# Pairing the column chunks of the input projections anew in a two-layer decoder trunk

## Chip, cores, metric

One core of one Trainium2 chip runs the whole program. The metric is device time in microseconds (us), from the program's start to its end; the kernel before took 2420.99 us, the median of three runs (2418.62 to 2423.28).

## What is computed

The reference is a trunk of two layers on an input of 256 rows by 2048 channels, all in float32:

```python
for l in range(DEPTH):
    h = rms_norm(x, mix_norm[l])
    proj = h @ w_in[l]                       # 2048 -> 7680 columns: q | k | v | u, v of the gating unit | gate logits
    q, k, v, uv, gate_logits = jnp.split(proj, cuts, axis=-1)
    branch_a = sliding_window_attention(...q, k, v...) @ w_attn_branch[l]
    branch_b = chunked_sgu(jax.nn.gelu(uv), ...) @ w_sgu_branch[l]
    gates = jax.nn.sigmoid(gate_logits)
    merged = gates[..., :D_MODEL] * branch_a + gates[..., D_MODEL:] * branch_b
    x = x + merged @ w_out[l]
    h2 = rms_norm(x, ffn_norm[l])
    x = x + (jax.nn.silu(h2 @ w_gate[l]) * (h2 @ w_up[l])) @ w_down[l]
```

The case is about `proj`, whose 7680 columns are computed in 15 chunks of 512: one with keys and attention values (`kv` 0), two of queries (`q` 0, 1), two of the gating unit's `v` ("values", `v` 0, 1), two of its `u` (`u` 0, 1), and eight of gate logits (`gate` 0 to 7).

## The kernel before

**A product in three parts.** Every float32 operand is split into a high part and a remainder (`hi` and `lo` of a weight, `uh` and `ul` of an activation), and a product is the sum of high times high, high times remainder and remainder times high. `add_product` (L361, L362) issues these: 3 matmuls of 512 columns for each 128 rows of the contraction. ScalarE makes `hi` (L261), VectorE makes `lo` as the difference (L262).

**Entries.** The work of TensorE is a list of entries made before anything is issued. A usual entry is one weight tile of 256 contraction rows by 512 columns, used for both halves of the 256 activation rows: 2 x 2 x 3 = 12 matmuls. A chunk with contraction length 2048 is 8 such entries.

**Single or pair.** `single` makes a plan of one chunk: 8 entries, 96 matmuls. `pair` makes a plan of two chunks A and B. There the first two weight tiles of A and of B form a 2 x 2 block product with the activation halves, and that is computed by the scheme of Winograd and Strassen with 7 products in place of 8: entries P1, P5, P2, P6, P7, P4 (the head) and P3, with 6 matmuls each, 42 in place of 48. Four of them need a difference of weight tiles first (L246, a subtraction of whole tiles on VectorE), all seven need a split, and partial sums go through a tile called `kept`: ScalarE copies one bank out (L384), one bank to another (L385), VectorE adds to `kept` twice (L387), and ScalarE writes `kept` back into the banks of B (L390, two copies). The other six weight tiles of A (entries G) and of B (entries U) are usual entries. A pair is thus 7 x 6 + 12 x 12 = 186 matmuls in 19 entries; two singles are 192 matmuls in 16 entries.

**Order.** The six head entries of a pair are put between the last six entries of the plan ahead of it:

```python
order = [t[0], h[0], t[1], h[1], t[2], t[3], h[3], h[2], t[4], h[4], t[5], h[5]]
```

where `t` are those six and `h` is P1, P5, P2, P6, P7, P4. TensorE's order is fixed by the program; the order on the other engines is worked out by a planner that runs the program against a model of time, with edges that put some steps behind the newest weight split.

**Lead.** `Stream.next` runs ahead of TensorE: loads are asked for 7 entries ahead, splits are made 4 entries ahead, differences 6 entries ahead. There are 5 buffers for raw tiles of usual entries, one buffer for each of the four raw tiles of a block (`k11`, `k12`, `k21`, `k22`), and 4 buffers each for `hi` and `lo`.

**Steps by slots.** Everything else is hung on a clock of slots. A unit is one weight tile against 128 of the 256 activation rows, and a slot passes with every two units: one usual entry is a slot, a P entry is half a slot (`debt`). `after(n, fn)` runs a step n slots later. Queries: normalising and rotating them takes 5 steps on VectorE, then `turn` (L431) transposes 32 x 32 blocks on VectorE and moves them with 16 DMAs (L437), for keys and queries on the queue of SyncE (SP), the queue of all weight loads; ScalarE copies the result to `qT` (L791). Scores and value products of the attention have fixed slots after the first query chunk. Values (`Spatial.v`) are evicted by ScalarE (L878); 4 slots after `v` 1 comes a GELU over both chunks, then four normalising steps 6 slots apart. `Spatial.u` has its GELU 7 slots after `u` 1, and 3 and 9 slots later the mixing (`psg`, L942) reads the normalised values of chunk 0 and of chunk 1.

**Banks.** Plans of the input projection use four PSUM banks, two for A and two for B. A pair that follows a pair uses A's banks again as soon as they are evicted.

**First part.** `FIRST_PART` lists, for each layer, the plans of the first twelve chunks in order. Before, in layer 0: `kv` 0, `q` 0, `q` 1, `gate` 0, `v` 0, `v` 1 single, then (`gate` 1, `u` 0), (`u` 1, `gate` 2), (`gate` 3, `gate` 4). In layer 1 `q` 1 and `gate` 0 are a pair as well.

Of the kernel before, what the change touches and what calls it, by code (L numbers as in the profile page):

```python
# [54 lines left out]
U_GELU, U_MIX, U_TURN = 7, (3, 9), (32, 39)  # L55
VALUES = (34, 44), (54, 64)
LOAD_BY = (2, 4, 5, 5)
FIRST_PART = [[(("kv", 0),), (("q", 0),)] + early + [(("v", 0),), (("v", 1),), (("gate", 1), ("u", 0)), (("u", 1), ("gate", 2)),
                                                  (("gate", 3), ("gate", 4))]
              for early in ([(("q", 1),), (("gate", 0),)], [(("q", 1), ("gate", 0))])]  # L60


@with_exitstack
def hybrid_trunk(ctx: ExitStack, tc: tile.TileContext, x, mix_norm, w_in, q_norm, k_norm, sinks,
# [108 lines left out]
    for l in range(DEPTH):  # L173
        wl = w_in[l]

        def of_in(kind, c):
            o = {"kv": O_KV, "q": 0, "v": O_V, "u": O_U, "gate": O_GATE}[kind] + c * CW
            return wl[:, o:o + CW]

        for f in FIRST_PART[l]:  # L180
            plans.append((single if len(f) == 1 else pair)(("in", l), *(of_in(*c) for c in f)))
# [97 lines left out]
    def after(n, fn):  # L279
        steps.append((slot_no[0] + n, fn))  # L280
# [251 lines left out]
    def summed(units, c, at):  # L532

        uh, ul = units[c]
        flat = slot([P, 4, S], name="flat")
        nc.vector.tensor_tensor(out=flat, in0=uh.bitcast(F32), in1=ul.bitcast(F32), op=ALU.add)
        ss = slot([P, 4, 2, P], name="sums")  # L540
        a11, a12, a21, a22 = (flat[:, 2 * k:2 * k + 2, t * P:(t + 1) * P] for t in range(NT) for k in range(2))

        def sums(n):
            for o, x0, x1, op in ((0, a21, a22, ALU.add), (1, ss[:, 0], a11, ALU.subtract),
                                  (2, a11, a21, ALU.subtract), (3, a12, ss[:, 1], ALU.subtract))[2 * n:2 * n + 2]:
                nc.vector.tensor_tensor(out=ss[:, o], in0=x0, in1=x1, op=op)

        def finished():
            sh = slot([P, 4, 2, P], F32R, "sh")
            sl = slot([P, 4, 2, P], F32R, "sl")  # L550
            nc.scalar.activation(sh, ss, AF.Copy)
            nc.vector.tensor_tensor(out=sl, in0=ss, in1=sh.bitcast(F32), op=ALU.subtract)
            units[c] = (uh, ul, sh, sl)

        after(at[0], lambda: sums(0))
        after(at[1], lambda: sums(1))
        after(at[2], finished)
# [440 lines left out]
    for l in range(DEPTH):  # L998
# [29 lines left out]

        for chunks in FIRST_PART[l]:
            if chunks == FIRST_PART[l][-1]:  # L1030
                after(1, lambda: summed(att.attT, WINO, (1, 2, 4)))
# [108 lines left out]
```

## Time and profile before

| | |
|---|---|
| runs | 2418.62, 2420.99, 2423.28 us |
| profiled execution | span 2416.4 us from the first to the last instruction; the page gives no other time for it |
| mean granted TensorE clock | 1.000 |
| busy share | TensorE 100%, weight load 82%, VectorE 87%, ScalarE 63%, GpSimd 13% |
| matmuls | 10692 |
| HBM | 207 GB/s read over the span |

TensorE is PE in the rows, the loading of its weights PEld, VectorE DVE, ScalarE ACT, GpSimd POOL, and the sequencer of SyncE that issues the loads SPq. A group row ends with `busy, mean ns of one | idle time of the engine just before them, and what ended it`. A row of a stretch gives its length, then for each engine the busy time and how many instructions touch the stretch, the granted clock, the DMA share and GB/s. A row of waits gives us in total, how many, and the longest.

### The profile page before, as it was taken

To read this page: it belongs to the slowest core of one execution; us is meant where nothing else is said; L and a number is where in the kernel's file an instruction comes from. 1 tells how busy PE (TensorE), PEld (TensorE's weight loads), DVE (VectorE), ACT (ScalarE), POOL (GpSimd) and SP (SyncE) were. 2 spreads that over 40 slices of the span, in tenths; PEclk is the share of its full clock that TensorE was granted. 3 is DMA by queue.
4 is the path that set the end of the run, shared out by engine and by line. 5 is a ranking of instruction groups with operands and counts; after the bars stand their busy time and mean duration, and the time that the engine had idled before them with its cause. 6 is when DMAs were issued, how large, how long until landed. Compare 5 with 4: busy or idle time off the path is not lost.

```text
span 2416.4 us, 31069 instructions
## 1 busy us (share of the span) xinstructions
PE 2405.1 (100%) x10692; PEld 1970.7 (82%) x10692; DVE 2092.0 (87%) x2409; ACT 1532.4 (63%) x1932; POOL 303.4 (13%) x557
## 2 busy tenths in 40 slices
PE   9999999999999999999999999999999999999999
PEld 7877888888888888888888778888888888888887
DVE  7779787898999998799887897878889989998998
ACT  6477555576666675666665775555676666666665
POOL 1100001132110111001301000011311101110010
PEclk9999999999999999999999999999999999999999
DMA  8755678687677757776957557776867786677773
GB/s 287 233 167 164 178 204 251 221 264 239 191 238 228 239 179 223 245 225 178 293 177 260 174 160 197 215 223 227 269 219 232 213 258 204 199 231 229 235 223 138
DMA packets 285070, 527.16 MB, mean 218 GB/s; under 512 B 28208, under 2 KB 40080, under 8 KB 284912
## 3 DMA queue, kind: packets, MB, share of 16 engines
q1 hardware_dynamic: 263056, 486.36, 63.6%
q0 software_dynamic: 21536, 38.56, 6.2%
q8 instruction: 83, 1.36, 0.2%
q14 instruction: 75, 0.61, 0.1%
q10 hardware_dynamic: 320, 0.27, 0.0%
HBM read 483.66 MB, written 16.78 MB: 207 GB/s over the span
## 4 chain that ended last, share of the span: by engine, by line
PE 88%; DVE 4%; DMA 4%; issue 1%; ACT 1%; SPq 1%; POOL 0%; DVEq 0%; ACTq 0%
PE acc L361 58%; PE acc L362 29%; DVE wlo L262 2%; DMA raw<-in_w_up_dram 2%; DMA raw<-in_w_in_dram 1%; DMA tt<-box 1%; ACT whi L261 1%; DVE raw L246 1%; SPq L437 1%; PE psc L807 1%; PE po L859 0%; PE psg L942 0%; PE ppt L844 0%; PE pt L474 0%; POOL tt L437 0%
## 5 line engine op out<-in xcount | busy, mean ns | idle before, releaser
L261 ACT ACTIVATE whi<-raw 128x1024 fp32r<-128x1024 f32 (+1 forms) x1116 | 1166.6, 1058 | 786.3 <-PE acc L362 440.0
L262 DVE TENSOR_TENSOR wlo<-raw,whi 128x1024 fp32r<-128x1024 f32 (+1 forms) x1117 | 1343.5, 1216 | 269.3 <-ACT whi L261 255.3
L361 PE MATMUL acc<-whi,uh 128*128 128x512 f32 x2854 | 1116.7, 391 | 1.4 <-ACT uh L460 1.4
L361 PE MATMUL acc<-wlo,uh 128*128 128x512 f32 x2854 | 1113.3, 390 | 2.1 <-DVE wlo L262 1.3
L362 PE MATMUL acc<-whi,ul 128*128 128x512 f32 x2854 | 1112.1, 390 | 0.6 <-DVE ul L465 0.6
L361 PEld LDWEIGHTS acc<-wlo,uh 128*128 128x128 f32 x2854 | 536.0, 188 | 118.5 <-DVE wlo L262 6.6
L361 PEld LDWEIGHTS acc<-whi,uh 128*128 128x128 f32 x2854 | 535.9, 188 | 117.8 <-issue 4.9
L362 PEld LDWEIGHTS acc<-whi,ul 128*128 128x128 f32 x2854 | 535.9, 188 | 112.8 <-DVE ul L465 1.5
L437 POOL DMA_DIRECT2D tt<-box x464 | 228.0, 499 | 1202.6 <-DVE box L431 339.7
L246 DVE TENSOR_TENSOR raw<-raw,raw 128x1024 f32<-128x1024 f32 x292 | 355.5, 1218 | 5.2 <-DMA raw<-in_w_up_dram 2.9
L361 PE MATMUL acc<-wlo,sh 128*128 128x512 f32 x584 | 228.1, 391 | 2.0 <-DVE wlo L262 2.0
L361 PE MATMUL acc<-whi,sh 128*128 128x512 f32 x584 | 228.4, 391 | 0.0
L362 PE MATMUL acc<-whi,sl 128*128 128x512 f32 x584 | 227.5, 390 | 0.0
L361 PEld LDWEIGHTS acc<-wlo,sh 128*128 128x128 f32 x584 | 109.7, 188 | 26.3 <-DVE wlo L262 4.1
L361 PEld LDWEIGHTS acc<-whi,sh 128*128 128x128 f32 x584 | 109.7, 188 | 25.1 <-issue 2.3
L362 PEld LDWEIGHTS acc<-whi,sl 128*128 128x128 f32 x584 | 109.6, 188 | 22.7
L387 DVE TENSOR_TENSOR kept<-acc,kept 128x512 f32<-128x512 f32 x102 | 69.6, 682 | 9.3 <-PE acc L362 9.3
L390 ACT ACTIVATE acc<-kept 128x512 f32<-128x512 f32 x102 | 59.7, 588 | 2.3 <-DVE kept L387 1.0
L964 POOL DMA_DIRECT2D held_x<-part x16 | 13.9, 868 | 301.4 <-ACT part L963 301.4
L333 POOL TENSOR_TENSOR rv<-ve,neg_half 128x4 f32<-128x4 f32 x8 | 10.2, 1273 | 266.8 <-DVE ve L907 247.9
L384 ACT ACTIVATE kept<-acc 128x512 f32<-128x512 f32 x51 | 30.1, 591 | 10.8 <-PE acc L362 10.5
L829 ACT ACTIVATE pr<-pr,negm 128x128 f32<-128x128 f32 x64 | 24.9, 390 | 16.0 <-DVE negm L820 16.0
(149 smaller groups left out, 909.0 us busy)
## 6 DMA issues: line engine op xcount, KB each, us to landing
raw<-in_w_in_dram SPq DMA_DIRECT2D x239, 512.0 KB, 4.8
raw<-in_w_gate_dram SPq DMA_DIRECT2D x176, 512.0 KB, 4.6
raw<-in_w_up_dram SPq DMA_DIRECT2D x176, 512.0 KB, 5.4
raw<-in_w_down_dram SPq DMA_DIRECT2D x176, 512.0 KB, 5.3
raw<-in_w_out_dram SPq DMA_DIRECT2D x64, 512.0 KB, 6.9
raw<-in_w_attn_branch_dram SPq DMA_DIRECT2D x64, 256.0 KB, 7.0
raw<-in_w_sgu_branch_dram SPq DMA_DIRECT2D x32, 512.0 KB, 5.8
tt<-box POOLq DMA_DIRECT2D x464, 32.0 KB, 4.7
```

The source lines that it names most:

```text
L246: self.last = nc.vector.tensor_tensor(out=self.raws[d], in0=self.raws[x], in1=self.raws[y], op=ALU.subtract)
L261: self.high = nc.scalar.activation(hi[:, i, :], raw[:, i, :], AF.Copy)
L262: self.last = nc.vector.tensor_tensor(out=lo[:, i, :], in0=raw[:, i, :], in1=hi[:, i, :].bitcast(F32), op=ALU.subtract)
L361: nc.tensor.matmul(ps, a, part[:, kk, :], start=first and kk + n == 0, stop=False, skip_group_check=True)
L362: nc.tensor.matmul(ps, b, hi[:, kk, :], start=False, stop=kk == 1, skip_group_check=True)
L384: nc.scalar.activation(p.kept[:, 1, :], a[0], AF.Copy)
L387: nc.vector.tensor_tensor(out=p.kept[:, int(tag == "P7"), :], in0=a[1], in1=p.kept[:, 1, :], op=ALU.add)
L390: nc.scalar.activation(ps, p.kept[:, t, :], AF.Copy)
L437: q.dma_start(dst[j * B:(j + 1) * B, i], box[i * B:(i + 1) * B, j])
L807: nc.tensor.matmul(pscore[:, i, :nk], self.qT[pair // 4][j * HD:(j + 1) * HD, pair % 4, t * P:(t + 1) * P], self.kT[j * HD:(j + 1) * HD, : ...
L829: self.exps = nc.scalar.activation(pr4[:, h, :], pr4[:, h, :], AF.Exp, bias=nm_[:, h:h + 1], accum_out=den[:, h:h + 1])
L964: nc.gpsimd.dma_start(held_x[j], part, accum_op=ALU.add)
```

## The change

In each layer's first part, `v` 0 is paired with `gate` 1 and `v` 1 with `u` 0. Before, `v` 0 and `v` 1 were single and `gate` 1 was paired with `u` 0. The other plans, and the functions, stay.

```diff
-FIRST_PART = [[(("kv", 0),), (("q", 0),)] + early + [(("v", 0),), (("v", 1),), (("gate", 1), ("u", 0)), (("u", 1), ("gate", 2)),
-                                                  (("gate", 3), ("gate", 4))]
-              for early in ([(("q", 1),), (("gate", 0),)], [(("q", 1), ("gate", 0))])]
+FIRST_PART = [
+    [(("kv", 0),), (("q", 0),), (("q", 1),), (("gate", 0),), (("v", 0), ("gate", 1),), (("v", 1), ("u", 0),), (("u", 1), ("gate", 2),), (("gate", 3), ("gate", 4),)],
+    [(("kv", 0),), (("q", 0),), (("q", 1), ("gate", 0),), (("v", 0), ("gate", 1),), (("v", 1), ("u", 0),), (("u", 1), ("gate", 2),), (("gate", 3), ("gate", 4),)],
+]
```

## The prediction

> **What bounds the kernel now.** I read the page's head first, then the cores' clock, the chain that ended last, and what TensorE waited for in the whole span.
>
> ```profile
> span 2416.4 us, 31069 instructions
> PE 2405.1 (100%) x10692; PEld 1970.7 (82%) x10692; DVE 2092.0 (87%) x2409; ACT 1532.4 (63%) x1932; POOL 303.4 (13%) x557
> core 0: 2416.4 us, clock 1.000
> PE 88%; DVE 4%; DMA 4%; issue 1%; ACT 1%; SPq 1%; POOL 0%; DVEq 0%; ACTq 0%
> PE acc L361 <- DVE wlo L262: 3.3, 5, 1.3
> PE acc L361 <- ACT uh L460: 1.4, 1, 1.4
> PE pwarm L312 <- DVE warm L307: 1.1, 1, 1.1
> PE acc L362 <- DVE ul L465: 0.6, 1, 0.6
> PE acc L361 <- DVE kept L387: 0.3, 1, 0.3
> ```
>
> TensorE is never without work for long: the five rows are all its waits, 6.7 us of 2416.4, and the clock is full. So a matmul that is taken out is worth its pitch, as long as the others go on supplying. What a matmul costs is not the mean in its group row, since that is a latency and neighbours overlap. The pitch comes from a long stretch that holds nothing but 512-column products:
>
> ```profile
> L361 PE MATMUL acc<-whi,uh 128*128 128x512 f32 x2854 | 1116.7, 391 | 1.4 <-ACT uh L460 1.4
> 500.00:880.00 380.00, 380.00 (x1677) 314.39 (x1676) 349.39 (x382) 249.51 (x290) 62.02 (x122) 1.00 0.73 229
> 880.00:920.00 40.00, 39.46 (x172) 31.66 (x171) 39.92 (x42) 26.90 (x31) 6.93 (x15) 1.00 0.57 172
> ```
>
> 380 us / 1677 = 0.2266 us, not 0.391. A usual entry (12 matmuls) lasts 2.72 us, a P entry (6) 1.36 us. The third row shows what happens where VectorE is full (39.92 of 40 us): TensorE gets 172 matmuls through; 40 / 0.2266 = 176.5, and with the two cut by the edges 178 would be whole, so some 6 matmuls or 1.4 us were lost.
>
> **What the change takes away and adds.** Each layer has one pair more and two singles less: 192 - 186 = 6 matmuls less per layer, 12 in all.
>
> - TensorE: 12 x 0.2266 = -2.72 us on the path that sets the end.
>
> The Trainium skill ("TensorE: Matmul & The Clock Gate", Back-to-back issue gap) gives about 131 ns for a matmul of 512 columns in a sustained stream; by that the term would be 12 x 0.131 = -1.6 us. The trace does not agree, with 227 ns over 1677 of them, and the trace decides.
>
> For the other engines the prices are these group rows:
>
> ```profile
> L262 DVE TENSOR_TENSOR wlo<-raw,whi 128x1024 fp32r<-128x1024 f32 x1113 | 1340.8, 1218 | 269.3 <-ACT whi L261 255.3 <-DMA kT<-box 2.0 <-DMA raw<-in_w_attn_branch_dram 1.6
> L246 DVE TENSOR_TENSOR raw<-raw,raw 128x1024 f32<-128x1024 f32 x292 | 355.5, 1218 | 5.2 <-DMA raw<-in_w_up_dram 2.9 <-DMA raw<-in_w_down_dram 1.7
> L387 DVE TENSOR_TENSOR kept<-acc,kept 128x512 f32<-128x512 f32 x102 | 69.6, 682 | 9.3 <-PE acc L362 9.3
> L261 ACT ACTIVATE whi<-raw 128x1024 fp32r<-128x1024 f32 x1113 | 1164.8, 1059 | 786.3 <-PE acc L362 440.0 <-DVE raw L246 207.1 <-issue 37.7
> L390 ACT ACTIVATE acc<-kept 128x512 f32<-128x512 f32 x102 | 59.7, 588 | 2.3 <-DVE kept L387 1.0 <-DVE gate L1037 0.6
> L384 ACT ACTIVATE kept<-acc 128x512 f32<-128x512 f32 x51 | 30.1, 591 | 10.8 <-PE acc L362 10.5
> L385 ACT ACTIVATE acc<-acc 128x512 f32<-128x512 f32 x51 | 29.9, 587 | 0.7
> ```
>
> - VectorE per layer: 4 differences and 3 more splits (7 P entries where 4 usual ones stood) at 1.218, 2 sums into `kept` at 0.682: 8.53 + 1.36 = 9.9 us, 19.8 us in all.
> - ScalarE per layer: 3 x 1.059 + 2 x 0.588 + 0.591 + 0.587 = 5.5 us, 11.1 us in all, on an engine that is 63% busy.
> - Loads: none. A pair reads 16 tiles of 512 KB, as two singles do; the SP queue has the same number of issues.
>
> **Where this work falls.** The old pair (`gate` 1, `u` 0) stood between `v` 1 and `u` 1; its place is taken by (`v` 1, `u` 0) at nearly the same matmul number. What is new in place is the head of (`v` 0, `gate` 1), which goes between the last six entries ahead of it. In layer 0 `gate` 0 is computed between the evictions of `q` 1 and of `gate` 0 on ScalarE (first two rows); its last six entries start two entries after 78.4 us, so the head stands at 84 to 115 us. In layer 1 they follow the eviction of `q` 1 (third row): 1284 to 1310 us.
>
> ```profile
> 78.58 0.69 ACT L1014 ACTIVATE q<-acc,rstd 128x512 f32<-128x512 f32 x1 [0.67 <-PE acc L362]
> 100.33 0.69 ACT L1014 ACTIVATE gate<-acc,rhalf 128x512 f32<-128x512 f32 x1 [0.67 <-PE acc L362]
> 1284.62 1.25 ACT L1014 ACTIVATE q<-acc,rstd 128x512 f32<-128x512 f32 x2
> 80.00:110.00 30.00, 30.00 (x142) 24.66 (x141) 23.57 (x29) 15.83 (x25) 3.58 (x2) 1.00 0.60 188
> 1280.00:1305.00 25.00, 25.00 (x112) 20.69 (x111) 20.58 (x21) 11.42 (x14) 3.54 (x2) 1.00 0.74 247
> 1236.00:1262.00 26.00, 26.00 (x116) 21.52 (x116) 23.09 (x28) 14.75 (x16) 2.56 (x1) 1.00 0.44 135
> ```
>
> Splits run some 4 entries ahead, so VectorE's share of the head falls into the stretches of the fourth and fifth rows. Layer 0: 23.6 + 9.9 = 33.5 us of work in 30 us, 3.5 too many. Layer 1: 20.6 + 9.9 = 30.5 us in 25 us, 5.5 too many, as both query chunks are rotated there. The last row is a head that exists, (`q` 1, `gate` 0) in layer 1: 23.1 of 26 us, and no wait of TensorE in it.
>
> What absorbs an excess is the lead of 4 splits, at most 4 x 2.72 = 10.9 us and 8.2 us where two of the four are P entries, less 1.06 + 1.22 us for the split itself. And the two rotations are not wanted at once, though their place in VectorE's order is the planner's. So the stall lies between 0 and 3.5 us in layer 0, between 0 and 5.5 us in layer 1. The nearest row is that of 880 to 920 us, VectorE full and 1.4 us lost. I take 0 in layer 0, where the excess is below the lead, and 1.4 us in layer 1.
>
> Layer 1 already loses something there, for another reason:
>
> ```profile
> 1288.34 12.85 SPq L437 DMA_DIRECT2D tt<-box  x16
> 1301.29 8.37 SPq L235 DMA_DIRECT2D raw<-in_w_in_dram  x7
> 1302.54 1.15 ACT L791 ACTIVATE qT<-tt 128x512 f32<-128x512 f32 x2 [5.78 <-DMA tt<-box]
> 1305.22 1.06 ACT L261 ACTIVATE whi<-raw 128x1024 fp32r<-128x1024 f32 x1 [0.38 <-DMA raw<-in_w_in_dram]
> 1307.59 0.50 PE L361 MATMUL acc<-wlo,uh 128*128 128x512 f32 x1 [0.68 <-DVE wlo L262]
> 77.72 11.28 SPq L437 DMA_DIRECT2D tt<-box  x16
> ```
>
> The 16 DMAs of the queries' turn hold SP for 12.85 us, so weight loads wait behind them; ScalarE stands 5.78 us before `qT`, with the splits queued behind it; the next split waits for a load issued after the turn, and TensorE waits 0.68 us. With the head there, six of the twelve entries take their tile from the `k` buffers, filled earlier, so the five raw buffers last longer: this load comes in time. I count the 0.7 us as gone. What the head worsens at this spot is ScalarE's stop: 5.8 + 1.2 + 1.2 (`qT` and eviction) + 2.3 = 10.5 us without a new split against a lead of 10.9 before and 8.2 then. That gives up to 2.3 us of stall; the 1.4 us taken stands for it too, since it is the same splits that are late. In layer 0 (last row; ScalarE's waits for `qT` are shorter, 4.06 us the longest) the same sum is 7.6 us, within 8.2.
>
> ```profile
> 111.83 1.15 ACT L791 ACTIVATE qT<-tt 128x512 f32<-128x512 f32 x2 [4.06 <-DMA tt<-box]
> ```
>
> **What is moved.** Counted in slots of layer 0: `v` 0 is finished at 40 in place of 39, `gate` 1 at 49 in place of 56, `v` 1 at 56 in place of 49, `u` 0 at 64 as before. The number of finished tiles held is the same at each time, so room in SBUF is short by `kept` alone, for some 8 slots. The GELU of the values and their four steps come 7 slots later; the last ends 25 slots after `v` 1, at 81, and the mixing of chunk 1 reads it at 87: 6 slots or 16 us to spare, where there were 14 slots. The steps move away from the scores in slots 37 to 57 and towards those at 62 and 67: no cost taken. A's banks of (`v` 0, `gate` 1) must be evicted within one U entry, 2.72 us, before P1 of the next pair writes them. An eviction of two banks took 1.25 us (the row at 1284.62), but behind a score's exponentials in ScalarE's order it can be late by up to 2 us in layer 1, where a score's slot falls two entries ahead; the existing pairs in a row show no such wait, so 0.
>
> The odd seventh P entry shifts all steps between the two first parts by half a slot, 1.36 us, against the products. This can open or close any of the few waits above: 0, bounds -1 and +2 us.
>
> **Sum.** -2.72 (matmuls) + 1.4 (stall) - 0.7 (late load gone) = -2.0 us, span 2414.4. The runs' median lies 4.6 us above the profiled span; carried over, 2420.99 - 2.0 = 2419.0 us.
>
> **Rivals.**
>
> 1. The lead absorbs all, and the late load vanishes: -2.72 - 0.7 = -3.4, 2417.6 us; if the half slot closes another wait, up to -6, 2415 us. For it: the head at 1236 us without a wait. Against: there VectorE had 3 us to spare, here it has none. Chance 0.20.
> 2. VectorE becomes the bound in the new heads. Place: the stretches 80 to 110 and 1280 to 1305 us; price: the whole excess, 3.5 + 5.5 = 9.0 us, -2.72: +6.3, 2427.3 us; it decides from the point where VectorE's backlog passes the lead, about 6 us. Part of it, from 5 us on, is already slower than before. Against: 880 to 920 us, where a full VectorE cost 1.4 us. By the Trainium skill ("Perfetto Trace Analysis", Identifying the Most-Contended Engine) TensorE is judged by weight-load time and VectorE by occupancy; with 82% against 87% the change loads the most contended engine, which is this rival. The trace so far speaks against the rule: TensorE's waits come to 0.3%. Chance 0.15.
> 3. The saving is given back outside: the half-slot shift opens waits of about 2 us, as the planner's orders change: 2421 us. For it: five waits on `wlo` stand in the trace at places where VectorE is near full. Chance 0.20.
>
> The forecast has 0.45, with a range of its own of 2417.5 to 2421.
>
> **Range and chances.** The spread of the three runs, 4.7 us, puts some 1.5 us on a median. About 0.2% (4.8 us: 2416.2 and 2425.8) is what a measurement can tell from no change. Below it lie about half of rival 1 and a little of the forecast: 0.13. Above it two thirds of rival 2 and a little of rival 3: 0.12. The rest, 0.75, is no difference. The range that leaves out 2 in 10 is 2415 to 2425.
>
> **What would show it.** Instructions: PE 10680, VectorE 18 more, ScalarE 14 more, L246 x300, L387 x106. TensorE's waits in layer 0 up to 120 us unchanged; the wait at 1307 us replaced by one of 1 to 2 us on `wlo` between 1290 and 1312 us. VectorE over 95% busy in both stretches. Rival 2 would show as 3 us or more of waits on `wlo` in each head; rival 3 as new waits after 300 us. Wrong altogether would be the pitch argument, if the span fell by 4.7 us (12 x 0.391) with the same waits; or the lead, if scores (L807) rather than splits were late, as the queries' rotation was pushed back.

## The result and the profile after

The changed kernel takes 2440.45 us (median of four runs, 2439.78 to 2442.07) against 2420.52 us for the kernel before (four runs): a ratio of 1.0085 with an interval of 1.0070 to 1.0099. It is slower by 20 us where 2 us less were forecast, and far outside the range. All lines of the code between L57 and the end have moved down by one, so the split is now L262 and L263, the difference L247, the copies of the banks L385 and L386, the sum into `kept` L388.

The head of the page after, and two of its groups:

```profile
span 2437.8 us, 31099 instructions
PE 2408.4 (99%) x10680; PEld 1971.3 (81%) x10680; DVE 2109.9 (87%) x2427; ACT 1549.6 (64%) x1948; POOL 306.3 (13%) x557
...
L247 DVE TENSOR_TENSOR raw<-raw,raw 128x1024 f32<-128x1024 f32 x300 | 366.0, 1220 | 4.7 <-DMA raw<-in_w_up_dram 2.4
...
L388 DVE TENSOR_TENSOR kept<-acc,kept 128x512 f32<-128x512 f32 x106 | 72.6, 685 | 10.3 <-PE acc L363 10.3
```

The work itself is what was counted: 12 matmuls fewer, 18 instructions more on VectorE, the groups as large as forecast. What TensorE waited for is new. The five largest rows of its waits in the whole span give us in total, how many, and the longest:

```profile
PE acc L362 <- ACT acc L386: 11.9, 3, 5.5
PE acc L362 <- DVE wlo L263: 4.1, 6, 1.6
PE acc L362 <- DVE kept L388: 2.2, 4, 0.8
PE acc L362 <- ACT q L1015: 1.8, 1, 1.8
PE acc L362 <- ACT u L879: 1.6, 1, 1.6
```

The first row stands nowhere in the kernel before. It is three waits for the copy from one bank to another that ScalarE makes after P5.

Where the time went is read by stretches. The first 300 us hold the first part of layer 0; then come the middle, up to the first part of layer 1, and that part. The two rows after:

```profile
300.00:1250.00 950.00, 936.57 (x4115) 772.19 (x4114) 822.86 (x880) 597.95 (x707) 141.52 (x276) 0.99 0.73 224
1250.00:1530.00 280.00, 275.45 (x1250) 219.43 (x1249) 232.98 (x328) 184.13 (x275) 18.37 (x9) 1.00 0.62 186
```

The same two stretches before:

```profile
300.00:1233.00 933.00, 932.16 (x4113) 768.70 (x4112) 821.03 (x879) 595.72 (x707) 142.51 (x276) 1.00 0.74 228
1233.00:1510.00 277.00, 276.32 (x1258) 221.11 (x1257) 224.60 (x319) 175.94 (x266) 15.77 (x9) 1.00 0.62 189
```

The middle, in which nothing was edited, needs 950 us in place of 933 for the same 4,100 matmuls, with 880 against 879 instructions on VectorE and 707 on ScalarE in both. That is 17.0 of the 21.4 us by which the two spans differ. Set matmul against matmul by their starts, the changed kernel is 0.3 us behind at the end of layer 0's first part, 17 us at the start of layer 1, 20.3 us at the end of its first part, and 21.4 us at the end. So the edited parts themselves cost 0.3 and 3.4 us where 1.36 us were to be won in each, and what remains is 1 us.

### The profile page after: what moved, and what is told of

It reads as the page before. It is cut to its first block, busy times and chain, and to the rows that moved or that the text cites. A ratio compares the mean times of both kernels' runs of the same rounds, so it can differ in the third digit from the quotient of the medians.

```text
span 2437.8 us, 31099 instructions
## 1 busy us (share of the span) xinstructions
PE 2408.4 (99%) x10680; PEld 1971.3 (81%) x10680; DVE 2109.9 (87%) x2427; ACT 1549.6 (64%) x1948; POOL 306.3 (13%) x557
## 3 DMA queue, kind: packets, MB, share of 16 engines
q8 instruction: 83, 1.36, 0.2%
## 4 chain that ended last, share of the span: by engine, by line
PE 86%; DVE 6%; DMA 2%; issue 2%; ACT 2%; SPq 1%; POOL 0%; DVEq 0%; ACTq 0%
PE acc L362 57%; PE acc L363 28%; DVE wlo L263 3%; DVE raw L247 1%; DMA raw<-in_w_in_dram 1%; ACT whi L262 1%; DMA raw<-in_w_up_dram 1%; SPq L438 1%; PE psc L808 0%; PE po L860 0%; DMA tt<-box 0%; DVE box L432 0%; DVE kept L388 0%; PE psg L943 0%; POOL rq L334 0%
## 5 line engine op out<-in xcount | busy, mean ns | idle before, releaser
L262 ACT ACTIVATE whi<-raw 128x1024 fp32r<-128x1024 f32 (+1 forms) x1122 | 1176.1, 1060 | 804.8 <-PE acc L363 463.4
L263 DVE TENSOR_TENSOR wlo<-raw,whi 128x1024 fp32r<-128x1024 f32 (+1 forms) x1123 | 1354.3, 1219 | 272.2 <-ACT whi L262 258.5
L247 DVE TENSOR_TENSOR raw<-raw,raw 128x1024 f32<-128x1024 f32 x300 | 366.0, 1220 | 4.7 <-DMA raw<-in_w_up_dram 2.4
L362 PE MATMUL acc<-whi,sh 128*128 128x512 f32 x600 | 236.5, 394 | 12.3 <-ACT acc L386 11.9
L362 PE MATMUL acc<-wlo,sh 128*128 128x512 f32 x600 | 235.7, 393 | 2.8 <-DVE wlo L263 2.8
L363 PE MATMUL acc<-whi,sl 128*128 128x512 f32 x600 | 235.0, 392 | 0.0
L388 DVE TENSOR_TENSOR kept<-acc,kept 128x512 f32<-128x512 f32 x106 | 72.6, 685 | 10.3 <-PE acc L363 10.3
L385 ACT ACTIVATE kept<-acc 128x512 f32<-128x512 f32 x53 | 31.3, 590 | 10.4 <-PE acc L363 10.1
L1077 ACT ACTIVATE hid<-acc,rstd 128x512 f32<-128x512 f32 x44 | 28.7, 683 | 10.2 <-PE acc L363 10.2
```

The costliest lines, as they stand in the source:

```text
L247: self.last = nc.vector.tensor_tensor(out=self.raws[d], in0=self.raws[x], in1=self.raws[y], op=ALU.subtract)
L262: self.high = nc.scalar.activation(hi[:, i, :], raw[:, i, :], AF.Copy)
L263: self.last = nc.vector.tensor_tensor(out=lo[:, i, :], in0=raw[:, i, :], in1=hi[:, i, :].bitcast(F32), op=ALU.subtract)
L362: nc.tensor.matmul(ps, a, part[:, kk, :], start=first and kk + n == 0, stop=False, skip_group_check=True)
L363: nc.tensor.matmul(ps, b, hi[:, kk, :], start=False, stop=kk == 1, skip_group_check=True)
L385: nc.scalar.activation(p.kept[:, 1, :], a[0], AF.Copy)
```

## The wait that opened

The first of the three waits stands at 440 us, in the output projection's pair of chunks 0 and 1. TensorE after, with the wait in brackets:

```profile
440.05 0.39 PE L363 MATMUL acc<-whi,ul 128*128 128x512 f32 x1
444.53 0.80 PE L362 MATMUL acc<-whi,sh 128*128 128x512 f32 x1 [4.08 <-ACT acc L386]
445.12 0.63 PE L362 MATMUL acc<-wlo,sh 128*128 128x512 f32 x1
445.55 0.63 PE L363 MATMUL acc<-whi,sl 128*128 128x512 f32 x1
```

ScalarE at this place in the timeline after (start, duration, and in brackets how long it stood and for whom):

```profile
442.31 1.06 ACT L262 ACTIVATE whi<-raw 128x1024 fp32r<-128x1024 f32 x1 [3.84 <-DVE raw L247]
443.28 0.58 ACT L385 ACTIVATE kept<-acc 128x512 f32<-128x512 f32 x1
443.89 0.58 ACT L386 ACTIVATE acc<-acc 128x512 f32<-128x512 f32 x1
```

ScalarE before:

```profile
437.05 0.60 ACT L384 ACTIVATE kept<-acc 128x512 f32<-128x512 f32 x1 [0.24 <-PE acc L362]
437.54 1.05 ACT L261 ACTIVATE whi<-raw 128x1024 fp32r<-128x1024 f32 x1
438.49 0.59 ACT L385 ACTIVATE acc<-acc 128x512 f32<-128x512 f32 x1
440.72 2.01 ACT L261 ACTIVATE whi<-raw 128x1024 fp32r<-128x1024 f32 x2 [1.64 <-DVE raw L246]
```

Before, the two copies go ahead of the split that has to wait for a difference; after, they stand behind it. The split waits 3.84 us, the copies behind it are ready all the while, and TensorE needs the copied bank for P6. At the two other places the copies stand behind other work. At 531 us it is a split that stands 1.65 us for TensorE's own matmuls. At 904 us, where the wait is longest, splits that stood 1.89 and 1.21 us for differences go first, and an eviction (`hid`) and a split of an activation (`uh`) go between the two copies.

At 440 us the difference is late because of VectorE's own order, here after, with a transpose, a step of the gate (L1053) and two remainders ahead of it:

```profile
437.51 0.71 DVE L432 STREAM_TRANSPOSE box<-gate 128x512 f32<-128x512 f32 x1
438.14 0.65 DVE L1053 TENSOR_TENSOR gate<-gate,gate 128x512 f32<-128x512 f32 x1
438.71 2.35 DVE L263 TENSOR_TENSOR wlo<-raw,whi 128x1024 fp32r<-128x1024 f32 x2
440.98 1.22 DVE L247 TENSOR_TENSOR raw<-raw,raw 128x1024 f32<-128x1024 f32 x1
```

Before, it starts 1.6 us earlier:

```profile
439.42 1.21 DVE L246 TENSOR_TENSOR raw<-raw,raw 128x1024 f32<-128x1024 f32 x1
```

VectorE has no more work in this stretch than before. It is busy for 15.00 of 15 us, after:

```profile
431.00:446.00 15.00, 10.82 (x44) 8.25 (x44) 15.00 (x17) 6.38 (x7) 1.75 (x4) 0.95 0.33 91
```

and before:

```profile
431.00:446.00 15.00, 15.00 (x68) 12.31 (x67) 15.00 (x18) 8.51 (x10) 4.21 (x9) 1.00 0.28 78
```

The waits of the middle come to 13.1 us after (11.9 for the copy, 0.8 and 0.4 for splits) against 0.4 before, 12.7 us of the 17. Most of the rest is the clock: behind the waits of 4.1 and 5.5 us it is granted at about half, and 7 and 12 matmuls come 0.43 us apart in place of 0.2266 (rows at 445.12 and 445.55 above), some 4 us together. The stretches that hold them, the granted clock being the third number from the end:

```profile
444.00:448.00 4.00, 3.47 (x8) 2.78 (x9) 2.64 (x3) 0.98 (x2) 3.75 (x8) 0.57 0.85 213
910.00:916.00 6.00, 5.74 (x14) 4.55 (x15) 1.68 (x2) 1.52 (x3) 0.00 (x0) 0.54 0.00 0
```

## The experiments

**Theories.** S: the odd seventh P entry of each new pair shifts every later step by half a slot against the products; steps of the middle then fall on other entries, the planner writes another order, and the three waits open. Its rival B (rival V in the expectations below): the new pairs leave VectorE or the buffers behind in some lasting way, and the shift has no part in it. Half a slot is one unit of the slots' clock, so it can be given back, or taken away, alone.

**Give half a slot back after each first part.** The changed kernel, with

```diff
+        def half_slot():
+            debt[0] += 1
+            if debt[0] >= 2:
+                debt[0] -= 2
+                tick()
+
+        half_slot()
```

behind the loop over the first part.

> The changed kernel, with half a slot given back after the first part of each layer, so that every later step falls on the same entry and the same slot as before the change; pairs as changed. Theory S (the half-slot shift between the two first parts makes the stalls there): the 16.6 us lost between the layers' first parts go, 0.3 us of layer 0's and 3.4 us of layer 1's first part stay: 2420.5 + 3.7 = about 2424 us (2422 to 2427), no wait of TensorE on the copy of the bank between 300 and 1250 us. Rival V (the longer work lists of VectorE and ScalarE, or a planner that is thrown off by any pair more): stays near 2440 us, with the same waits.

2427.19 us (ratio to the kernel before 1.0032, 1.0019 to 1.0045; here and below the ratio is to runs of the kernel before taken beside it, with medians of 2418.2 to 2419.8 us). The waits for the bank's copy are gone from the middle; 2.1 us of others are left there, the largest of 1.2 us at 346 us, for the sums into `kept`. Theory S holds for the larger part; the time came out just above the range that it expected.

**Shift the kernel before, with no new pair.** Half a slot is taken away after layer 0's first part and given back ahead of layer 1's; in a second kernel it is given first and taken away later.

```diff
+        if l == 0:
+            debt[0] -= 1
```

> The kernel before, pairs as before, with half a slot taken away after the first part of layer 0 and given back ahead of the first part of layer 1. No product, load or split more or less. Theory S: the same waits on the bank's copy as in the changed kernel, at about 440, 531 and 904 us, 2420.5 + 16.6 = about 2437 us (2434 to 2440). Rival V: 2420.5 us, as no pair is added.

> The kernel before with half a slot too many, in place of too few, between the first part of layer 0 and that of layer 1: every step comes half a slot early, not late. Theory S by position (what counts is which entry a step falls on, and early or late by half a slot is the same entry): the same waits on the bank's copy as with half a slot too few, about 2437 to 2442 us. Rival by lateness (steps that come later starve TensorE): 2420 us or less.

2442.66 us (1.0091, 1.0076 to 1.0106) and 2439.07 us (1.0082, 1.0066 to 1.0097). The first of the two came out above its range. Both show the same waits as the changed kernel. The first row of TensorE's waits in the middle is the same in both:

```profile
PE acc L361 <- ACT acc L385: 11.9, 3, 5.5
```

The stretch of the middle in the second kernel:

```profile
300.00:1250.00 950.00, 935.97 (x4100) 770.91 (x4099) 820.69 (x876) 594.81 (x706) 140.86 (x276) 0.99 0.71 224
```

The whole loss of the middle thus comes without any of the change's work. It is even larger: matmul against matmul, the shifted kernels lose 19.5 and 19.9 us between the two first parts, the changed kernel 16.6. Some 2 us of these 3 are the clock again, which was slow for more matmuls behind waits of the same length. Steps half a slot early and half a slot late do the same harm, so it isn't lateness: it is on which entry a step falls. In the rest of layer 1, where the changed kernel's two halves have added up to a whole slot, it lost only 1 us. B is out for the middle.

**Each layer alone**, with half a slot given back behind its first part.

> The new pairs in layer 0 alone, with the half slot given back after its first part; layer 1 as before. Theory S: 2420.5 + 0.3 = about 2421 us (2419 to 2423): 1.4 us of matmuls saved, 1.7 us of small waits. Rival V: most of the loss stays, as it all stood between the first parts: about 2437 us.

> The new pairs in layer 1 alone, with the half slot given back after its first part; layer 0 as before. Both theories have layer 1's own cost here: 2420.5 + 3.4 = about 2424 us (2422 to 2426), with waits of TensorE on the eviction of queries 1 and of u in the first part of layer 1. If it is 2420 us or less, those waits came from the shifted slots as well.

Layer 0 alone: 2422.45 us (1.0012, 1.0003 to 1.0021). Layer 1 alone: 2424.00 us (1.0017, 1.0007 to 1.0026), with a wait of 2.1 us for the eviction of queries 1. The wait for the eviction of `u` that was expected too is not there. Neither layer is ahead of the kernel before, even without the waits for the bank's copy.

**Is it ScalarE's order?** The changed kernel without any slot given back, but the splits that follow P5 in the program are kept behind its copies:

```diff
+                    elif self.hold is not None:
+                        with tc.issue_after(self.hold.ins):
+                            self.high = nc.scalar.activation(hi[:, i, :], raw[:, i, :], AF.Copy)
...
-            nc.scalar.activation(a[0], a[1], AF.Copy)
+            stream.hold = nc.scalar.activation(a[0], a[1], AF.Copy)
```

> The changed kernel, half slot not given back, with one edge more in ScalarE's order: the weight splits that are emitted after a pair's two P5 copies stay behind these copies (before, the planner could put them ahead). No instruction more or less. Theory O (the stalls are ScalarE's order: the copy stands behind a split that waits for VectorE's difference): the three waits on the bank's copy, 11.9 us, and the slow matmuls behind them go; the loss between the first parts falls from 16.9 to 2 to 5 us, 2440.5 - 13 = about 2427 us (2424 to 2430). Rival L (VectorE is simply late there, so that TensorE would wait for the split or the sum next): the wait only changes its name to wlo or kept, over 2435 us.

2430.89 us (1.0049, 1.0032 to 1.0066), just above what was expected. ScalarE in the timeline of this kernel at the place of the first wait (lines stand 2 to 4 further down here):

```profile
437.85 0.60 ACT L389 ACTIVATE kept<-acc 128x512 f32<-128x512 f32 x1 [0.24 <-PE acc L367]
438.48 0.58 ACT L390 ACTIVATE acc<-acc 128x512 f32<-128x512 f32 x1
...
442.77 2.01 ACT L264 ACTIVATE whi<-raw 128x1024 fp32r<-128x1024 f32 x2 [2.75 <-DVE raw L248]
```

The largest of TensorE's waits in its middle:

```profile
PE acc L366 <- DVE wlo L267: 2.4, 4, 0.8
PE acc L366 <- ACT acc L390: 1.9, 1, 1.9
PE acc L366 <- ACT uh L461: 1.7, 1, 1.7
```

The copies now go first, the split still waits, and the middle loses 7 us where it lost 17. So about 10 us, slow clock included, came from the copies' place behind a waiting split. The other 7 stand in the rows above: remainders from VectorE, a copy that is late for another reason, and a split of an activation. The same edge in the kernel before, where the copies go ahead of the waiting split in any case, changes nothing that can be measured in the time: 2420.14 us (1.0006, 0.9996 to 1.0015). Its profile does show a price: 3.1 us of waits in the middle, for remainders and splits of activations, where the kernel before has 0.4. So the copies' place may have cost somewhat more than the 10 us that the edge gave back.

> The kernel before with the same edge in ScalarE's order. Theory O: no wait on the copy was there, so 2420 us, within 3 us either way. Rival: the edge by itself speeds up or slows down by more, which would spoil the reading of the run on the changed kernel.

**Where to give the half slot back.** Later, when the attention's branch is gated (about 340 us in layer 0), and earlier, directly behind the pair of `v` 0 and `gate` 1:

```diff
+        debt[0] += 1
+        if debt[0] >= 2:
+            debt[0] -= 2
+            tick()
```

> The changed kernel with the half slot given back in each layer after the attention branch is gated (at about 340 and 1565 us) in place of right after the first part, so that steps set in the first part and due soon after it are not moved. If the 1.4 us waits at 344 and 1552 us in the run with the early correction came from there, they go: about 2424 us (2422 to 2426); else 2427 us as there. The wait on the eviction of queries 1 in layer 1 (2.6 us) stays.

> The changed kernel with the half slot given back right after the pair of values 0 and gate 1, in the middle of the first part of each layer. By theory S any place ahead of 430 us removes the 16.6 us between the layers; what differs is only which steps set earlier move by half a slot: 2424 us (2421 to 2428). A loss of over 10 us against before would speak against S.

Late: 2423.39 us (1.0021, 1.0012 to 1.0031). Early: 2424.59 us (1.0024, 1.0013 to 1.0034), with a wait of 1.5 us for the eviction of `u`. That wait shows here and in the changed kernel, not with layer 1 alone nor with the late place, so it seems to go with where the slots stand in the first part and not with the new pairs as such. With the late place the middle is as in the kernel before, with one wait of 0.4 us and this row of the stretch, 933 us for 4119 matmuls:

```profile
300.00:1233.00 933.00, 932.31 (x4119) 770.01 (x4118) 821.90 (x880) 596.63 (x708) 142.59 (x276) 1.00 0.72 229
```

And still it is slower than before, by 5 us. Here the first part of layer 1 can be read without the shift. TensorE's waits in it from 1233 to 1513 us:

```profile
PE acc L362 <- ACT q L1015: 2.3, 1, 2.3
PE acc L362 <- DVE kept L388: 1.4, 3, 0.9
PE acc L362 <- DVE wlo L263: 0.7, 2, 0.4
```

VectorE, then ScalarE, in its timeline at the first of them:

```profile
1282.72 1.22 DVE L755 TENSOR_TENSOR q<-q,ca 128x1024 f32<-128x1024 f32 x1
1283.86 1.66 DVE L247 TENSOR_TENSOR raw<-raw,raw 128x1024 f32<-128x1024 f32 x1
...
1285.63 2.00 ACT L262 ACTIVATE whi<-raw 128x1024 fp32r<-128x1024 f32 x2 [3.03 <-DVE raw L247]
1287.55 1.25 ACT L1015 ACTIVATE q<-acc,rstd 128x512 f32<-128x512 f32 x2
```

It is the same pattern once more. The difference for P5 of the new head stands on VectorE behind the rotation of queries 0; the split of it waits 3.03 us on ScalarE; behind that split stands the eviction of queries 1; and P1 of the new head needs the bank. 4.4 us of waits stand where the kernel before has 0.7.

**Take the two causes of this wait away.** Once by edges that keep the splits behind the eviction of a pair's first chunk too, beside the copies-first edge and the late half slot:

> The late correction, the edge behind the P5 copies, and the same edge behind the eviction of a pair's first chunk in the input projections. Theory O: the wait of 2.6 us on the eviction of queries 1 in layer 1 goes as well, as its eviction stood behind a split waiting for the new P5 difference: 2.5 us below the run with the late correction alone, about 2421 us (2418 to 2424). If the difference itself is what is late, TensorE waits for the split of P5 instead and nothing is won.

2423.44 us (1.0021, 1.0012 to 1.0030): the wait for the eviction is gone, but TensorE waits 3.7 us for splits, four times, 2.1 us at most. Nothing is won in all. The longest of the four is not at the late difference, as the expectation had it, but 18 us later in the head, at 1306 us. There a split stands on ScalarE behind the copy of the turned queries, which itself stands for its DMAs:

```profile
1302.10 1.16 ACT L798 ACTIVATE qT<-tt 128x512 f32<-128x512 f32 x2 [1.80 <-DMA tt<-box]
1303.16 1.04 ACT L264 ACTIVATE whi<-raw 128x1024 fp32r<-128x1024 f32 x1
```

Once by leaving out, in the kernel with the late half slot, three of the five steps that rotate the queries of layer 1 (its output is then that of unrotated queries):

```diff
-                after(1 + i, step)
+                if step not in left:
+                    after(1 + i, step)
```

> The changed kernel with the late correction of the half slot; in layer 1 both query chunks are left unrotated (three of the five steps on VectorE left out, 3.8 us per chunk, between some 1280 and 1305 us), so VectorE has 7.6 us less to do beside the new head. Theory D (VectorE is short there: the P5 difference is late, and the eviction of queries 1 behind it): the wait of 2.3 us on that eviction and the waits on wlo at 1304 to 1311 us shrink to under 1 us in all; layer 1's first part no longer loses 2.5 us against before but gains about 1: 2423.4 - 3.5 = about 2420 us (2418 to 2422). Rival Q (the load queue behind the DMAs of the turn, or ScalarE's order alone): the waits stay, 2423 us.

2424.65 us (1.0023, 1.0014 to 1.0032), though 7.6 us of VectorE's work are gone just there: a miss for the theory that the rotation sets the loss. The wait for the eviction did go, as it said. But ScalarE's copy of the turned queries now goes ahead of two splits and stands 5.07 us for its DMAs, with the splits behind it. ScalarE in the timeline with the late half slot alone, where the copy follows the splits:

```profile
1300.88 1.06 ACT L262 ACTIVATE whi<-raw 128x1024 fp32r<-128x1024 f32 x1 [0.30 <-PE acc L363]
1302.19 1.16 ACT L792 ACTIVATE qT<-tt 128x512 f32<-128x512 f32 x2 [0.25 <-DMA tt<-box]
```

and without the rotation:

```profile
1300.43 1.15 ACT L794 ACTIVATE qT<-tt 128x512 f32<-128x512 f32 x2 [5.07 <-DMA tt<-box]
1301.48 1.99 ACT L262 ACTIVATE whi<-raw 128x1024 fp32r<-128x1024 f32 x2
```

and the first row of TensorE's waits from 1233 to 1513 us:

```profile
PE acc L362 <- DVE kept L388: 4.0, 2, 3.2
```

VectorE is not full here: it is busy for 19.2 us between 1280 and 1305 us, where it has 24.5 with the late half slot alone, and stands 4.8 us for a split. So this head has at least two places where something that is ready stands behind something that waits, and in both runs taking the first away brought out the second. An order that avoids both was not found; what the new pairs of layer 1 are worth with one stays open.

**The best that could be put together**: new pairs in layer 0 alone, the late half slot, both edges.

> The version that the runs point to: new pairs in layer 0 alone, the half slot given back late, and splits kept behind the P5 copies and the eviction of a pair's first chunk. Theory S with O: layer 0's first part gains some 0.5 to 1 us of its 1.4, nothing is lost later: 2418 us (2416 to 2421), beside 2418 to 2420 of before; not told apart from before is the likeliest. Rival: the edges cost as much as in the run on the kernel before, 2 us: 2421.

2419.84 us (1.0005, 0.9996 to 1.0014). It can't be told from the kernel before, and no version tried is faster than that.

## Why the prediction was wrong, point by point

- **The half slot: the step that failed.** "The odd seventh P entry shifts all steps between the two first parts by half a slot ... 0, bounds -1 and +2 us." The step was seen and its mechanism named (rival 3, new waits after 300 us, 2421 us). Its size was 17 us in the changed kernel, and 22 and 20 us when the kernel before was shifted alone (+0.91% and +0.82%). The bound came from the largest existing waits of the kernel before, 0.3 to 1.4 us. Those are what is left after an order that fits; they don't say what an order costs that does not fit. That order cost up to 5.5 us at one place, as work that is ready stands behind a waiting instruction, and then a slower clock on top.
- **Layer 1's head.** The stall was taken as 1.4 us, and 0.7 as won back. Measured: waits of 4.6 us in the changed kernel (1.8, 1.6, 0.8 and 0.4) and 4.4 us with the late half slot, against 0.7 before. The step that gave "0" for the eviction of the banks looked at `v` 0 alone and for a score ahead of it; the bank that came late was that of queries 1, behind a split that waited for a difference. The 1.6 us for the eviction of `u` seem to go with the shifted slots (above). The wait of 0.68 us at 1307 us is gone, as forecast, in so far as no split stands for a load there; one of 0.39 us for a remainder stands at much the same place, 1324 us.
- **Layer 0's head.** Taken as 0; the first part ended 0.3 us behind instead of 1.36 ahead, 1.7 us lost, of which 1.0 us shows as waits for `kept` (0.4 at 109 us, in the head, and 0.6 at 207 us, behind it). The lead did absorb most of it.
- **VectorE full in both heads.** Forecast over 95%, as 9.9 us more of work were put into each stretch. Measured 94% and 98%, with 4.6 and 4.0 us more, in the changed kernel's stretches that answer to 80 to 110 and 1280 to 1305 us before:

```profile
80.00:110.00 30.00, 29.59 (x139) 24.15 (x138) 28.21 (x31) 19.11 (x23) 4.48 (x2) 1.00 0.57 179
1297.00:1322.00 25.00, 23.23 (x102) 18.60 (x100) 24.53 (x27) 14.65 (x18) 6.26 (x2) 1.00 0.67 221
```

- **Rival 2, VectorE as the bound there (+6.3 us).** Not as such: with the rotation left out, 7.6 us less work for VectorE, the loss stayed, with VectorE no longer full. One of the two waits did go with that work, so VectorE's load has a part in it; how large a part beside the order is not shown.
- **What was right.** The counts of instructions on PE, VectorE and of L247 and L388 (ScalarE has 16 more, 14 were counted), and loads that are no more than before. The pitch holds too: the middle less its waits and the slow clock, 950 - 13.1 - 4 us, divided by 0.2266 gives 4117 matmuls, and the row counts 4115.

## What to carry to other kernels

Where other work hangs on a clock that counts units of the main work, an edit that changes the count by an odd part moves everything downstream, in stages that it does not touch; shift the old kernel alone by that part, and the price is known before the edit is argued over. Small waits in a tuned order are no bound on what another order costs: look at each in-order queue for what stands behind an instruction that waits, above all where the main engine wants it. A busy share does not tell: VectorE had 15.00 of 15 us in both kernels, with no wait in one and 4.1 us in the other.

## What the runs showed of the hardware

The price of a long wait is more than its length: behind waits of 4.1 and 5.5 us the granted clock was 0.57 and 0.54 in the stretches shown, and the next 7 and 12 matmuls came 0.43 us apart, some 1.4 and 2.4 us more than at full clock. The Trainium skill ("TensorE: Matmul & The Clock Gate", Part 1: The HAM clock gate) says that the clock halves after an idle window of about 3.4 us and comes back after about as long under load. For these two waits the trace agrees on the halving; the clock was back after some 3 and 5 us (7 and 12 matmuls). It does not set the bound at 3.4 us: a wait of 2.3 us at 531 to 534 us was followed by full clock in the changed kernel and by about half in the kernel before with half a slot taken away. The stretch in the changed kernel:

```profile
533.90:538.00 4.10, 4.06 (x18) 3.36 (x19) 4.10 (x5) 1.99 (x3) 4.10 (x9) 1.00 0.72 200
```

and in the shifted kernel:

```profile
533.90:538.00 4.10, 4.02 (x11) 3.16 (x12) 3.44 (x5) 1.28 (x3) 4.10 (x10) 0.58 0.75 202
```

So a wait of 2.3 us can cost the clock or not; what decides it was not tried. Nor does the length alone set the price: behind the wait of 4.1 us, 7 matmuls were slow in the changed kernel and 12 in the kernel before with half a slot given first.
